# Residual adds of the down projection as accumulating DMAs, and one more block-product pair in the up projection

## The chip, the cores and the metric

The kernel runs on one NeuronCore of a Trainium2 chip. The metric is the device time of one execution in microseconds. The core has a matrix engine (TensorE, PE in the profile, with its weight loads as PEld), a vector engine (VectorE, DVE), a scalar engine (ScalarE, ACT), a general engine (GpSimd, POOL) and a queue that mostly issues DMAs (SyncE, SP). Each works through its own instructions in the order in which they were issued, and they meet at semaphores. Matrix products land in PSUM, everything else lives in SBUF.

## The reference

Two layers of an encoder trunk on 512 tokens of width 1024, all in float32. The first half of each layer (a gated recurrence, a spatial gate and a windowed attention, merged and added to `x`) is not touched. What matters is the second half:

```python
        hn = rms_norm(x, ln2[l])
        x = x + jnp.square(jax.nn.relu(hn @ w_up[l])) @ w_down[l]
    return rms_norm(x, final_norm)
```

`w_up` is 1024 x 4096 and `w_down` 4096 x 1024 per layer.

## The kernel before

**Precision.** Every operand of a float32 product is split into a high part `hi` (rounded to the matrix engine's fast float32 type) and a rest `lo`, and each product is three matmuls (`hi*hi`, `lo*hi`, `hi*lo`). For weights `wsplit` (L201) does this: `hi` is a ScalarE cast (L203), `lo` a VectorE subtraction (L204), both 128 x 1024, into one of `WB` = 3 pairs of buffers (`whl`, L197). `split` (L255) does the same for activations (L258, L259).

**The MLP in quarters.** The 4096 hidden features of a layer are taken in four quarters `qd` (loop at L1244). A quarter has an up part and a down part, and each hands its tiles to the next.

*Up*: eight tiles of 128 features, taken as four pairs `j`. A plain pair is two calls of `proj` (L212): per tile 8 x 3 matmuls of 512 columns with one split weight chunk, then Relu and Square on ScalarE (L1269, L1270). A block pair is one call of `up_pair` (L493): the two tiles together are a 2 x 2 block product done with seven block products instead of eight. Each has 4 x 3 matmuls of 256 columns, 84 in all. It has to form sums of the two raw weight chunks first (L499, L500, L503, L505, all VectorE, 512 wide), splits four weight tiles instead of two (three of 1024 columns, one of 512), and puts its results together with three VectorE adds (L529, L535, L537). `PAIRS[qd]` and `AHEAD[qd]` (L89) say which pairs are block products: none in quarter 0, pair 1 (whose weights are loaded ahead, into the `wq` buffers) and pair 2 (loaded into the `wr` buffers, of which there are `WR` = 2) in quarters 1 to 3. After each pair `left_first` and `left_second` (L360, L368) make the sums and splits of the hidden tiles that the down part needs.

*Down* (`down`, L471, through `seven`, L422): the quarter's 512 x 1024 hidden block times a 1024 x 1024 block of `w_down`, again as seven block products, in the order 1, 2, 6, 7, 5, 4, 3. Each is 24 matmuls of 512 columns into two PSUM banks (p = 0, 1). Before products 6, 5 and 4 VectorE forms sums of raw weight chunks in place (L447, L449, L451), two each. Later products add to what an earlier one left in the same bank (6, 5 and 3 on the banks of 1; 4 on those of 7), so each intermediate result has to be read out before the next product on that bank begins. The reading out is `on` (L474): one VectorE instruction per bank (L478), which takes the PSUM bank, multiplies it by the row scale `r2` (or its negative) and adds it to the residual tile `xr[t][fl]` in SBUF. There are 14 of these in a quarter. In quarter 3 `done` follows, which begins the next norm and the stores.

**Order.** The program is written once in plain order; a planner built into the framework lists the instructions of each engine by priority and by when its own model has their inputs ready. `hp()` raises a block's priority; among raised ones the earlier in the text goes first. The order on each engine is then fixed.

**Queues.** SP issues all weight loads (512 KB each). POOL issues the other loads and stores, and DMAs that do arithmetic; the descriptors of POOL's DMAs are kept in a strip of SBUF whose size the last function of the kernel sets (`dynamic_dma_scratch_size`, not given before).

Of the kernel before, what the change touches and what calls it, by code (L numbers as in the profile page):

```python
# [9 lines left out]
AF = mybir.ActivationFunctionType  # L10
ALU = mybir.AluOpType
# [48 lines left out]
def trunk(tc, xT, xt, ws, vec, fnb, bsb, snk, wst, rope, cmask, amask, ident, out):  # L60
    nc = tc.nc
# [3 lines left out]
    def pool(**kw):  # L65
# [15 lines left out]
             "yh": 8,  # L81
             "q": 2, "a": 8, "g": 2, "ch": 7,
             "yi": 16, "th": 8,
             "h": 18, "xm": 8}

    HOME = {t: p for p, ts in {"G": ("xs", "zt"), "Y1": ("yh",), "br": ("q", "a", "g", "ch"), "Y2": ("yi", "th"), "mlp": ("h", "xm")}.items() for t in ts}
    part = {}
    BANKS = {"m": 2, "a": 2, "c": 2, "s": 2}
    PAIRS, AHEAD = ((), (2,), (2,), (2,)), ((), (1,), (1,), (1,))  # L89
    GROUPS = (("m", "m", "c", "c"), ("a", "a", "s", "s"))  # L90
    WR, WB, NZ, NSM, NQ = 2, 3, 2, 3, 8

    CTS = {2: 5, 3: 4}

    def nm(s):
        ctr[0] += 1
        return f"{s}_{ctr[0]}"

    def T(tag, name, dt=F32):
        where = part[HOME[tag]] if tag in HOME else sb  # L100
        return where.tile([P, S], dt, tag=tag, bufs=SLOTS[tag], name=nm(name))
# [17 lines left out]
    def PT(tag, name):  # L119
        return ps.tile([P, S], F32, tag="p_" + tag, bufs=BANKS[tag], name=nm(name))  # L120
# [44 lines left out]
    pt = PT("s", "idle")  # L165
# [46 lines left out]
    def proj(xs, name, *key, bank="m"):  # L212

        return proj_w(xs, name, wload(*key), bank=bank)
# [256 lines left out]
    def down(qd, raw, hs, xr, r2, nr2, done, between, last):  # L471
        V = nc.vector

        def on(which, p, pt):  # L474
            t, fl, sign = {"P1": (p, 0, 1), "P2": (p, 0, 1), "P16": (2 + p, 0, 1), "P7": (2 + p, 1, -1),
                           "P165": (2 + p, 1, -1), "P74": (2 + p, 0, 1), "P1653": (p, 1, -1)}[which]
            r = r2 if sign > 0 else nr2
            V.scalar_tensor_tensor(xr[t][fl], pt, r[:, t:t + 1], xr[t][fl], ALU.mult, ALU.add)  # L478
            if qd == 3 and which in ("P2", "P165", "P74", "P1653"):
                done(t, fl)  # L480

        seven(raw, hs, "d", on, between=between, apart=last and qd == 3)
# [292 lines left out]
    for i in range(8):  # L775
        t = T("zt", "xt")
# [9 lines left out]
    for l in range(DEPTH):  # L786
        xs = n1.xs
# [164 lines left out]
        for g in range(4):  # L952
            pt = PT("s", "mx")
# [64 lines left out]
        pt = PT("c", "vT")  # L1018
# [69 lines left out]
        def gates(tag, i, fl):  # L1088

            res = []  # L1090
            for t in range(4):
                z = T(tag, "gt")
                nc.gpsimd.dma_start(z, thd[:, i * 4 + t, fl * S:(fl + 1) * S])
                res.append(z)
            return res
# [34 lines left out]
        with later(30000):  # L1130
# [5 lines left out]
            for fl in range(2):  # L1136
                th = gates("ch", 0, fl)
# [31 lines left out]
        for fl in range(2):  # L1169
            th, mc = tha[fl], mcs[fl]  # L1170
# [9 lines left out]
        xr = [[T("l", "xr"), T("l", "xr")] for _ in range(4)]  # L1180
# [47 lines left out]
        def done(t, fl):  # L1228

            n1.add(t, fl)  # L1230
            if not last:
                nc.gpsimd.dma_start(xspill[:, t, fl * S:(fl + 1) * S], xr[t][fl])
            if last:

                if fl == (t > 1):
                    nc.vector.tensor_tensor(xr[t][fl], xr[t][fl], fn_t[fl], ALU.mult)
                if (t, fl) in ((0, 1), (1, 1)):
                    finish((t,))
                elif (t, fl) == (3, 0):
                    finish((2, 3))  # L1240
            elif t % 2:
                n1.turn(fl, (t - 1, t))

        for qd in range(4):  # L1244
# [10 lines left out]
            for j in range(4):  # L1255
                if j in PAIRS[qd] or j in early:
                    us = up_pair(*(early.get(j) or pair_load(keys(j), False)), hx, "s" if j % 2 else "m")
                for i in range(2):
# [3 lines left out]
                    else:  # L1262
                        pt = proj(n2.xs, f'up{qd}', l, "up", qd, f, bank="s" if f % 4 > 1 else "m")
# [156 lines left out]
```

## Time and profile before

| | us |
|---|---|
| median of 3 runs | 1645.81 |
| lowest and highest run | 1644.52, 1646.4 |
| span of the profiled execution | 1644.4 |
| PE busy in it | 1631.2 (99%) |
| DVE, ACT, POOL busy in it | 1358.9 (83%), 1012.9 (62%), 102.4 (6%) |

The profile is that of one execution; its span counts from the first to the last instruction, and lies 1.4 us under the median of the runs. In the profile a matmul is shown with the time from its start to the end of its pipeline, so matmuls overlap, and what a matmul costs is the distance from one start to the next. VectorE instructions overlap their neighbours by a little in the same way. The eight quarters of the two layers lie at 495.3 to 821.2 us (layer 0) and 1312.1 to 1636.4 us (layer 1).

### The profile page before, as it was taken

The page shows a single profiled execution, that of the slowest core. Times are in us where ns is not written, and L with a number is a line of the kernel's source. Part 1 is how long each engine was busy: PE and PEld are TensorE (multiplying, and loading weights), DVE is VectorE, ACT ScalarE, POOL GpSimd, SP SyncE. Part 2 cuts the span into 40 slices and gives each one's busy share as a digit, 9 for nine tenths or more (in the row PEclk, how much of TensorE's full clock was granted, in tenths as well). Part 3 has the DMA queues.
Part 4 walks back from the last instruction along what each step waited for, and adds up shares of the span by engine and source line. Part 5 has one row for each costly group of instructions (what it writes and reads, how often), then busy time and mean ns, then how long its engine had stood idle before and what let it go on. Part 6 is the DMA issues. An engine that isn't in the chain of part 4 may idle for free. (4 is left out here: it accounts for less than half of the span.)

```text
span 1644.4 us, 24323 instructions
## 1 busy us (share of the span) xinstructions
PE 1631.2 (99%) x9137; PEld 1376.8 (84%) x9137; DVE 1358.9 (83%) x2183; ACT 1012.9 (62%) x1731; POOL 102.4 (6%) x165
## 2 busy tenths in 40 slices
PE   9999999999999999999999999999999999999998
PEld 7788888888888898989888888888887888989896
DVE  7888979677758988898989869887877589898887
ACT  7667567677247564646666555886862464647374
POOL 0012000000300000000010110000003000000001
PEclk9999999999999999999999999999999999999999
DMA  8343222222625333232423432223226343232311
GB/s 309 102 154 125 78 90 73 102 97 85 236 92 190 100 106 103 103 115 91 141 90 125 144 121 78 77 91 105 92 86 232 106 162 117 89 128 77 129 65 52
DMA packets 55590, 191.55 MB, mean 116 GB/s; under 512 B 7376, under 2 KB 7632, under 8 KB 55472
## 3 DMA queue, kind: packets, MB, share of 16 engines
q1 hardware_dynamic: 44352, 154.43, 27.3%
q0 software_dynamic: 10688, 35.00, 5.8%
q8 instruction: 72, 1.18, 0.3%
q10 hardware_dynamic: 432, 0.55, 0.1%
q14 instruction: 46, 0.38, 0.1%
HBM read 173.18 MB, written 16.78 MB: 116 GB/s over the span
## 5 line engine op out<-in xcount | busy, mean ns | idle before, releaser
L203 ACT CAST wh<-wq 128x1024 fp32r<-128x1024 f32 x214 | 225.2, 1053 | 205.1 <-PE dA L434 60.9
L204 DVE TENSOR_TENSOR wl<-wq,wh 128x1024 fp32r<-128x1024 f32 x214 | 260.4, 1221 | 62.8 <-ACT wh L203 60.3
L203 ACT CAST wh<-wr 128x1024 fp32r<-128x1024 f32 x164 | 172.0, 1049 | 155.1 <-PE wo L251 27.5
L204 DVE TENSOR_TENSOR wl<-wr,wh 128x1024 fp32r<-128x1024 f32 x164 | 199.9, 1220 | 61.0 <-ACT wh L203 55.1
L210 PE MATMUL up<-xh,wl 128*128 128x512 f32 x320 | 124.8, 390 | 0.0
L209 PE MATMUL up<-xl,wh 128*128 128x512 f32 x320 | 124.8, 390 | 0.0
L208 PE MATMUL up<-xh,wh 128*128 128x512 f32 x320 | 124.6, 391 | 0.0
L434 PE MATMUL dA<-wh,sh 128*128 128x512 f32 x256 | 99.8, 390 | 0.0
L433 PE MATMUL dA<-wh,sh 128*128 128x512 f32 x256 | 98.5, 390 | 0.0
L435 PE MATMUL dA<-wl,sh 128*128 128x512 f32 x256 | 91.9, 389 | 0.0
L656 DVE TENSOR_TENSOR ex<-ex 128x512 f32<-128x512 f32 x112 | 74.9, 686 | 3.5 <-ACT kt L647 3.2
L208 PEld LDWEIGHTS up<-xh,wh 128*128 128x128 f32 x320 | 60.1, 188 | 12.4
L210 PEld LDWEIGHTS up<-xh,wl 128*128 128x128 f32 x320 | 60.1, 188 | 12.3
L209 PEld LDWEIGHTS up<-xl,wh 128*128 128x128 f32 x320 | 60.1, 188 | 12.2
L644 ACT ACTIVATE qt<-ex 128x512 f32<-128x512 f32 x56 | 37.9, 677 | 33.8 <-DVE ex L656 31.8
L433 PEld LDWEIGHTS dA<-wh,sh 128*128 128x128 f32 x256 | 48.1, 188 | 10.0
L434 PEld LDWEIGHTS dA<-wh,sh 128*128 128x128 f32 x256 | 48.1, 188 | 9.9
L435 PEld LDWEIGHTS dA<-wl,sh 128*128 128x128 f32 x256 | 48.1, 188 | 9.9
L523 PE MATMUL us<-xs,wh 128*128 128x256 f32 x192 | 54.1, 283 | 0.0
L522 PE MATMUL us<-xs,wh 128*128 128x256 f32 x192 | 54.1, 283 | 0.0
L524 PE MATMUL us<-xs,wl 128*128 128x256 f32 x192 | 53.4, 283 | 0.0
L208 PE MATMUL gz<-xh,wh 128*128 128x512 f32 x128 | 50.9, 398 | 0.0
(435 smaller groups left out, 4780.6 us busy)
## 6 DMA issues: line engine op xcount, KB each, us to landing
wr<-in_ws_dram SPq DMA_DIRECT2D x158, 512.0 KB, 3.5
wq<-in_ws_dram SPq DMA_DIRECT2D x124, 512.0 KB, 4.3
thd<-zt POOLq DMA_DIRECT2D x32, 256.0 KB, 2.5
gt<-thd POOLq DMA_DIRECT2D x32, 256.0 KB, 3.9
mgd<-mg POOLq DMA_DIRECT2D x16, 256.0 KB, 2.3
mB<-mgd POOLq DMA_DIRECT2D x16, 256.0 KB, 6.7
x<-in_xT_dram SPq DMA_DIRECT2D x8, 256.0 KB, 7.5
xt<-in_xt_dram SPq DMA_DIRECT2D x8, 256.0 KB, 8.3
```

The lines of the kernel that those rows point to most:

```text
L203: nc.scalar.copy(hi, raw)
L204: nc.vector.tensor_tensor(lo, raw, hi.bitcast(F32), ALU.subtract)
L208: nc.tensor.matmul(pt, whi, xhi, start=first, stop=False)
L209: nc.tensor.matmul(pt, whi, xlo, start=False, stop=False)
L210: nc.tensor.matmul(pt, wlo, xhi, start=False, stop=last)
L433: nc.tensor.matmul(pt, xh[:, t], hi[:, c], start=start and k == 0, stop=False, skip_group_check=True)
L434: nc.tensor.matmul(pt, xl[:, t], hi[:, c], start=False, stop=False, skip_group_check=True)
L435: return nc.tensor.matmul(pt, xh[:, t], lo[:, c], start=False, stop=k == 3, skip_group_check=True)
L522: nc.tensor.matmul(pt, hi[:, c], xh, start=n in (1, 2, 7) and k == 0, stop=False, skip_group_check=True)
L523: nc.tensor.matmul(pt, hi[:, c], xl, start=False, stop=False, skip_group_check=True)
L524: nc.tensor.matmul(pt, lo[:, c], xh, start=False, stop=k == 3, skip_group_check=True)
L656: nc.vector.tensor_tensor(o_ap, o_ap, ap_of(ex, i_, [[istep, 2]] + z), ALU.add)
```

## The change

In quarters 0 to 2 of each layer the 14 results of a down part are no longer added to the residual by VectorE. ScalarE copies each PSUM bank with its scale into one of four new buffers `dx`, and a DMA issued from POOL adds that buffer to the residual tile. Quarter 3 is as it was. In quarters 1 to 3 pair 3 of the up part becomes a block pair as well (so pairs 1, 2 and 3 are), its weights loaded into the `wr` buffers, of which there are now 3. To make room in SBUF for `dx` (four tiles of 2 KB per partition) and the third `wr` (4 KB), the strip for POOL's DMA descriptors is set to 4 KB per partition.

```diff
-             "h": 18, "xm": 8}
+             "h": 18, "xm": 8, "dx": 4}
...
-    PAIRS, AHEAD = ((), (2,), (2,), (2,)), ((), (1,), (1,), (1,))
+    PAIRS, AHEAD = ((), (2, 3), (2, 3), (2, 3)), ((), (1,), (1,), (1,))
...
-    WR, WB, NZ, NSM, NQ = 2, 3, 2, 3, 8
+    WR, WB, NZ, NSM, NQ = 3, 3, 2, 3, 8
...
             r = r2 if sign > 0 else nr2
+            if qd < 3:
+                z = T("dx", "dx")
+                nc.scalar.activation(z, pt, AF.Copy, scale=r[:, t:t + 1])
+                nc.gpsimd.dma_start(xr[t][fl], z, accum_op=ALU.add)
+                return
             V.scalar_tensor_tensor(xr[t][fl], pt, r[:, t:t + 1], xr[t][fl], ALU.mult, ALU.add)
-            if qd == 3 and which in ("P2", "P165", "P74", "P1653"):
+            if which in ("P2", "P165", "P74", "P1653"):
                 done(t, fl)
...
-    nc = _bacc.Bacc("TRN2", target_bir_lowering=False, num_devices=1)
+    nc = _bacc.Bacc("TRN2", target_bir_lowering=False, num_devices=1, dynamic_dma_scratch_size=4096)
```

More of the change, by code (lines that the diff above doesn't have):

```diff
@@ L83, in trunk @@
              "yi": 16, "th": 8,
-             "h": 18, "xm": 8}
-    HOME = {t: p for p, ts in {"G": ("xs", "zt"), "Y1": ("yh",), "br": ("q", "a", "g", "ch"), "Y2": ("yi", "th"), "mlp": ("h", "xm")}.items() for t in ts}
+             "h": 18, "xm": 8, "dx": 4}
+    HOME = {t: p for p, ts in {"G": ("xs", "zt"), "Y1": ("yh",), "br": ("q", "a", "g", "ch"), "Y2": ("yi", "th"), "mlp": ("h", "xm", "dx")}.items() for t in ts}
     part = {}
     BANKS = {"m": 2, "a": 2, "c": 2, "s": 2}
-    PAIRS, AHEAD = ((), (2,), (2,), (2,)), ((), (1,), (1,), (1,))
+    PAIRS, AHEAD = ((), (2, 3), (2, 3), (2, 3)), ((), (1,), (1,), (1,))
     GROUPS = (("m", "m", "c", "c"), ("a", "a", "s", "s"))
-    WR, WB, NZ, NSM, NQ = 2, 3, 2, 3, 8
+    WR, WB, NZ, NSM, NQ = 3, 3, 2, 3, 8
     CTS = {2: 5, 3: 4}
```

## The prediction

> **What bounds the kernel now.** First the head of the page and its strip of 40 slices, then the list of what PE waited for.
>
> ```profile
> span 1644.4 us, 24323 instructions
> ...
> PE 1631.2 (99%) x9137; PEld 1376.8 (84%) x9137; DVE 1358.9 (83%) x2183; ACT 1012.9 (62%) x1731; POOL 102.4 (6%) x165
> ...
> DVE  7888979677758988898989869887877589898887
> ```
>
> ```profile
> PE idle L167 <- DVE idle L164: 1.6, 1, 1.6
> PE tA L435 <- DVE wl L204: 1.3, 1, 1.3
> PE wo L251 <- DVE mgl L259: 0.4, 2, 0.3
> ```
>
> PE is busy all the time and its longest waits are single ones in other stages: none lies on an up or a down matmul. So only PE work that goes away can shorten the MLP, and only a new PE wait can lengthen it. DVE is at 8 to 9 tenths in the MLP slices (13 to 20, 32 to 40): the engine that could make PE wait. Next, one late quarter of layer 1 by stretches (PE, PEld, DVE, ACT, POOL busy, clock, DMA share, GB/s): plain pair, block pairs 1 and 2, plain pair 3, products 1 and 2 of the down part; then the whole down parts of an earlier quarter and of the last.
>
> ```profile
> 1556.00:1566.90 10.90, 10.90 (x50) 9.03 (x49) 7.49 (x11) 3.20 (x6) 0.00 (x0) 1.00 0.25 94
> 1566.90:1577.00 10.10, 10.10 (x85) 10.07 (x84) 8.70 (x14) 6.99 (x12) 0.00 (x0) 1.00 0.32 105
> 1577.00:1587.70 10.70, 10.70 (x88) 10.55 (x87) 9.29 (x17) 9.17 (x17) 0.00 (x0) 1.00 0.31 98
> 1587.70:1598.20 10.50, 10.50 (x49) 8.69 (x48) 10.50 (x17) 7.43 (x15) 0.00 (x0) 1.00 0.16 52
> 1598.20:1609.00 10.80, 10.80 (x49) 8.97 (x48) 9.93 (x14) 6.94 (x9) 0.00 (x0) 1.00 0.00 0
> ...
> 620.90:659.00 38.10, 38.10 (x170) 31.57 (x169) 33.40 (x39) 17.57 (x20) 0.00 (x0) 1.00 0.34 113
> ...
> 1598.20:1636.40 38.20, 38.20 (x169) 31.32 (x167) 34.17 (x43) 20.59 (x32) 1.98 (x4) 1.00 0.01 2
> ```
>
> The reader is to see the fourth row: in the stretch of pair 3, which the change makes a block pair, DVE is already busy for all of its 10.50 us. It works off there what the two block pairs left behind.
>
> **What PE gains.** Three starts of that quarter: the plain pair, the first block pair, the down part.
>
> ```profile
> 1556.00 0.39 PE L208 MATMUL up<-xh,wh 128*128 128x512 f32 x1
> ...
> 1566.88 0.28 PE L522 MATMUL us<-xh,wh 128*128 128x256 f32 x1
> ...
> 1598.16 0.39 PE L433 MATMUL dA<-wh,sh 128*128 128x512 f32 x1
> ```
>
> A plain pair (48 matmuls) takes 1566.88 - 1556.00 = 10.88 us. From 1566.88 to 1598.16 are 31.28 us for two block pairs and one plain: (31.28 - 10.88) / 2 = 10.20 us for a block pair (84 matmuls). Making one more pair a block pair saves 0.68 us, and six of them (three quarters, two layers) 4.1 us, 0.25%. That is all that the change takes off PE; the DMAs and copies take no PE work away.
>
> **What DVE gets and loses.** DVE prices as the distance from one start to the next:
>
> ```profile
> 1573.30 1.22 DVE L204 TENSOR_TENSOR wl<-wr,wh 128x1024 fp32r<-128x1024 f32 x1
> 1574.43 0.69 DVE L259 TENSOR_TENSOR sh<-sf,sh 128x512 fp32r<-128x512 f32 x1
> 1575.04 0.69 DVE L499 TENSOR_TENSOR wr<-wr,wr 128x512 f32<-128x512 f32 x1
> 1575.64 0.41 DVE L535 TENSOR_TENSOR u<-u,us 128x256 f32<-128x256 f32 x1
> 1575.97 0.69 DVE L500 TENSOR_TENSOR wr<-wr 128x512 f32<-128x512 f32 x1
> ...
> 1578.37 0.69 DVE L259 TENSOR_TENSOR wl<-t,wh 128x512 fp32r<-128x512 f32 x1 [0.78 <-ACT wh L258]
> ```
>
> A `lo` of 1024 columns costs 1.13, a 512-wide sum or split 0.60, a 256-wide add 0.33 us. A block pair has, over a plain one, four sums (L499, L500, L503, L505) and one 512-wide split, 5 x 0.60 = 3.0; one more `lo`, 1.13; three adds, 1.0: 5.1 us more DVE work in each up part of quarters 1 to 3. What goes:
>
> ```profile
> 1599.22 1.23 DVE L204 TENSOR_TENSOR wl<-wq,wh 128x1024 fp32r<-128x1024 f32 x1 [0.87 <-ACT wh L203]
> ...
> 1600.72 1.22 DVE L451 TENSOR_TENSOR wq<-wq,wq 128x1024 f32<-128x1024 f32 x1
> 1601.85 0.42 DVE L383 SCALAR_TENSOR_TENSOR sf<-sf,u 128x256 f32<-128x256 f32 x1
> ...
> 1604.86 1.40 DVE L478 SCALAR_TENSOR_TENSOR xr<-dA,r,xr 128x512 f32<-128x512 f32 x2
> 1606.18 1.22 DVE L451 TENSOR_TENSOR wq<-wq,wq 128x1024 f32<-128x1024 f32 x1
> 1607.31 1.22 DVE L204 TENSOR_TENSOR wl<-wq,wh 128x1024 fp32r<-128x1024 f32 x1
> ```
>
> Two L478 cost 1.32, so 14 cost 9.2 us in each down part of quarters 0 to 2. That is more than comes, but in another place: it goes where PE did not wait, and work cannot be pulled forward to it, because `lo` needs one of three weight buffers, which PE frees at its own pace (the 0.87 us wait for a cast above is such a wait).
>
> So DVE enters the down part late, and the sharpest due time there is the weights of product 6. Its first `lo` (1607.31) ends at 1608.53, product 6 starts half a us later (1598.16 + 2 x 38.10 / 7 = 1609.05). In quarter 3 the lateness is 5.1 for the pair, plus 0.7 as PE comes earlier, less the 0.5 margin, less the 0.87 idle gap, less two L451 (2 x 1.13) that the planner can put behind, since only product 4 needs them: 2.2 us. Two splits of `left_second` may go behind too (0.9): 1.2 to 2.2 us. In quarters 1 and 2 the two L478 of product 1 are gone as well (1.32): 0 to 0.9. I take the middles, 0.4, 0.4 and 1.7 per layer, 5.0 us in both. After product 6 the last down part has work for DVE in 34.17 of 38.20 us and the others 9.2 less, so nothing later is due.
>
> **ScalarE, POOL and the DMAs.** The nearest rows for a copy out of PSUM, for DMAs from POOL, and for what POOL spends to issue one:
>
> ```profile
> L1269 ACT ACTIVATE u<-up x40: 582/590/606, 510.0 to 1599.1; 128x512 f32<-128x512 f32 x40
> ```
>
> ```profile
> thd<-zt POOLq DMA_DIRECT2D x32, 256.0 KB, 2.5
> ...
> mgd<-mg POOLq DMA_DIRECT2D x16, 256.0 KB, 2.3
> mB<-mgd POOLq DMA_DIRECT2D x16, 256.0 KB, 6.7
> ```
>
> ```profile
> L874 POOL DMA_DIRECT2D thd<-zt x32: 539/539/607, 83.8 to 963.7; - x32
> ```
>
> 14 copies of 0.59 are 8.3 us on ACT per down part: 17.57 becomes 26 of 38.10, which fits. A copy waits for its product's end; behind it in ACT's queue stand casts (L203) which wait for PE as well. I cost it at nothing; without that cover it is 1.2 us per product. The bank is needed again one product later at the earliest (38.10 / 7 = 5.44 us), so two copies have time. In the up part a block pair adds one and a half casts of 1024 columns and three copies of 256, at the 0.59 per 512 columns some 2.7 us, to ACT, which is the less loaded engine in every row above.
>
> No row shows an accumulating DMA. It moves 256 KB and reads its target too: from 2.3 us (a plain store) to 13.4 (twice the slowest load). I take 5.0, twice `thd<-zt`, the nearest in size and queue. Two DMAs on one residual tile must follow one another (products 1 and 2, 7 and 5), 5.44 us apart: 5.0 fits. Four `dx` tiles hold two products, 10.9 us: fits. POOL has nothing else in quarters 0 to 2, 14 issues of 0.54 fill 7.6 us of 38.1, and the next to touch the residual is the next quarter's down part, over 40 us later. The DMA engines are at 0.34. So zero, up to a landing time of 10.9 us. The third `wr` lets loads start earlier, in a place where PE does not wait: zero. The smaller strip matters only if POOL had to wait for room; at one DMA per 2.7 us I take zero.
>
> [...]
>
> **The rivals.**
>
> *A, DVE keeps up: faster.* DVE is idle for 1.4 us in each of the second and third stretches above (10.10 - 8.70, 10.70 - 9.29), 2.8 together, more than the 2.2 of quarter 3. If the new order fills those gaps, no due time is missed and the 4.1 us stay: 1641.7. Against it: those gaps wait for ACT casts inside a chain (the 0.78 above), and a third pair has the same chain.
>
> *B, PE waits inside the third pair: slower.* In 1577.0 to 1587.7 DVE worked 9.29 us. With a block pair next it must also make L499, L500 and L503 there (1.8 us): 11.1 us in 10.2, then comes the cast with its 0.78: 1.7 us late for the third pair's product 6. The `left` work of pair 2 comes first in the text, and if the planner puts part of it before that pair's last splits, more. It decides as soon as what DVE owes at the start of pair 3 is over 1 us. At 1.7 to 3 us in six quarters, 10 to 18 us, less 4.1: 1652 to 1660, most likely near its low end, 1653. The lateness at product 6 of the down part is then used up and not added.
>
> *C, the accumulating DMAs land late: slower.* Beyond 10.9 us a `dx` is not free, ACT stands still at the copy, and the casts behind it stop PE. At 13.4 us, 14 DMAs through 4 tiles need 47 us for a down part of 38: 9 us in six parts, +50, 1696. Against it: all POOL rows lie under 7 us. [...]
>
> **How the numbers follow.** The forecast: -4.1 + 5.0 = +0.9, 1645.3 for the profiled span and 1646.7 for the median, which lies 1.4 above it. Its own range is -4.1 + 2 x 1.2 = -1.7 to -4.1 + 2 x (0.9 + 0.9 + 2.2) = +3.9: 1644.1 to 1649.7. Chances: forecast 0.42, A 0.25, B 0.25, C 0.08. A measurement of this kernel tells about 0.2% (3.3 us) from no change. A gives 0.21 faster and 0.04 within (small losses are enough); the forecast 0.39 within and 0.03 slower; B and C 0.33 slower. So 0.21, 0.43, 0.36. The range runs from A with a little to spare, 1641, to the larger part of B, 1655; C and the end of B are left out.
>
> **What would show it.** PE has 9137 - 6 x 48 + 6 x 84 = 9353 matmuls. Right: waits of about 0.4 to 2 us of PE for DVE `wl` at the start of product 6 (second `dA` group), longest in quarter 3, and the three block pairs at 10.2 us each. A: no such waits. B: the waits stand at `us` in the third pair. C: ACT waits for a DMA on `dx`, and landings over 10 us. The prediction is wrong from the start if the order of the untouched stages shifts by more than a us or two.

## The result, and the profile after

| | before | after |
|---|---|---|
| median, us | 1645.6 | 1659.73 |
| lowest and highest run, us | 1644.52, 1646.4 | 1659.01, 1660.9 |
| span of the profiled execution, us | 1644.4 | 1659.1 |

The changed kernel is slower by 14.1 us: ratio 1.0088, 95% interval 1.0076 to 1.01. That lies outside the range given, above it. The head of the page of the changed kernel (busy time, share of the span and instructions of each engine):

```profile
span 1659.1 us, 25081 instructions
...
PE 1636.5 (99%) x9353; PEld 1384.5 (83%) x9353; DVE 1334.6 (80%) x2153; ACT 1074.4 (65%) x1851; POOL 174.7 (11%) x249
```

The amounts of work came out as worked out ahead: 9353 matmuls, and 1358.9 - 1334.6 = 24.3 us less busy time on DVE, against 6 x (9.2 - 5.1) = 24.6. Only the time went the other way. What PE waited for in the changed kernel (in total, times, longest):

```profile
PE us L529 <- DVE wl L204: 3.5, 6, 1.0
PE dB L433 <- ACT wh L203: 3.4, 6, 0.7
PE dC L433 <- ACT wh L203: 2.0, 1, 2.0
```

These three are new, are the longest and lie in the MLP: `us` L529 (the block pairs of the up part), `dB` (product 2 of the down part), `dC` (the banks of products 7 and 4, once). None of them stands at product 6 of the down part, where the prediction put the lateness. To see what each stage gained or lost, take the first matmul of a quarter and of the next: in the changed kernel, quarter 1 of layer 0,

```profile
577.27 0.39 PE L208 MATMUL up<-xh,wh 128*128 128x512 f32 x1
...
659.04 0.39 PE L208 MATMUL up<-xh,wh 128*128 128x512 f32 x1
```

and in the kernel before,

```profile
578.66 0.39 PE L208 MATMUL up<-xh,wh 128*128 128x512 f32 x1
...
658.96 0.39 PE L208 MATMUL up<-xh,wh 128*128 128x512 f32 x1
```

81.77 us against 80.30. In the same way, for all stages (us; "start" is what lies ahead of the first up part, "between" the untouched half of layer 1; the last quarter ends with the start of the last matmul, the tail with the span):

| | start | q0 | q1 | q2 | q3 | between | q0 | q1 | q2 | q3 | tail |
|---|---|---|---|---|---|---|---|---|---|---|---|
| before | 495.3 | 83.4 | 80.3 | 80.1 | 82.1 | 490.9 | 83.4 | 80.3 | 80.2 | 80.0 | 8.4 |
| after | 493.9 | 83.4 | 81.8 | 81.9 | 84.0 | 492.6 | 83.4 | 81.8 | 83.1 | 85.5 | 7.8 |

Quarter 0, which has the DMA adds and no block pair, is the same. The six quarters with a third block pair lose 1.5, 1.7, 2.0, 1.5, 2.9 and 5.5 us (from starts with two decimals), 15.0 together, where 4.1 were to be gained; the stretch between the layers loses 1.7; start and tail are 2.0 shorter.

**Where a quarter loses.** The changed kernel by stretches of quarter 1: block pairs 1, 2 and most of 3, then the start of the down part (PE, PEld, DVE, ACT, POOL busy, clock, DMA share, GB/s):

```profile
588.15:598.35 10.20, 10.20 (x86) 10.17 (x85) 8.77 (x14) 7.02 (x12) 0.00 (x0) 1.00 0.32 104
598.35:608.60 10.25, 10.25 (x86) 10.15 (x86) 9.21 (x17) 7.84 (x15) 0.00 (x0) 1.00 0.33 102
608.60:618.50 9.90, 9.48 (x75) 9.05 (x75) 9.90 (x17) 8.05 (x15) 0.00 (x0) 1.00 0.34 108
618.52:631.85 13.33, 12.64 (x61) 10.05 (x60) 13.18 (x20) 10.41 (x17) 0.85 (x1) 1.00 0.00 1
```

The reader is to see the third of the engine columns, DVE: 8.77, then 9.21, then 9.90 of 9.90. From the third block pair on DVE has no gap left, and there PE's column falls below the length for the first time. The instructions that waited there:

```profile
613.68 0.39 PE L529 MATMUL us<-xs,wl 128*128 128x256 f32 x1 [0.42 <-DVE wl L204]
...
618.60 1.05 ACT L203 CAST wh<-wq 128x1024 fp32r<-128x1024 f32 x1 [1.03 <-PE us L528]
...
621.77 1.05 ACT L203 CAST wh<-wq 128x1024 fp32r<-128x1024 f32 x1 [0.53 <-PE us L528]
...
622.87 0.50 PE L433 MATMUL dB<-wh,sh 128*128 128x512 f32 x1 [0.60 <-ACT wh L203]
```

First the third pair's product 7 waits for the `lo` of its weights. Then ScalarE cannot cast the down part's weights: each cast needs one of the three weight buffers, and waits for a matmul of the third pair (L528) to let go of it. The first of the two casts waits for the buffer of products 5 and 4. The second waits for that of products 7 and 3, and product 3 is the pair's last; PE starts it only at 620.27, after six matmuls of the down part's product 1. So PE waits again, for the cast of product 2. From one matmul's start to the next, less the usual spacing, PE loses some 0.6 us at product 7, 0.25 at product 1 (at 619.70, right behind the first of the two casts) and 0.9 at product 2. The whole quarter loses 1.47 + 0.68 = 2.15; the rest is in steps of about 0.1. Reckoned in the same way, quarter 2 of layer 0 loses 2.4, and quarters 1 and 2 of layer 1 lose 2.2 and 3.5. In the last of these, product 6 of the third pair waits 0.6 us for its `lo` as well, and product 7 waits 1.0.

**The last quarter.** What held `dC` up for 2.0 us in the last down part, in order of time:

```profile
1630.47 0.68 DVE L1241 TENSOR_TENSOR xr<-xr,fn 128x512 f32<-128x512 f32 x1
...
1631.07 1.22 DVE L449 TENSOR_TENSOR wq<-wq,wq 128x1024 f32<-128x1024 f32 x1
...
1632.38 1.99 ACT L203 CAST wh<-wq 128x1024 fp32r<-128x1024 f32 x2 [1.34 <-DVE wq L449]
...
1634.42 0.50 PE L433 MATMUL dC<-wh,sh 128*128 128x512 f32 x1 [2.02 <-ACT wh L203]
```

A weight sum (L449) stands on DVE behind the final norm's product (L1241), the first of the two casts waits for the sum, and PE for the second, which stands behind it. In the kernel before, this sum stands behind that product too, but there it ended 1.9 us before product 5 (PE, 1619.92), and here 0.9 us after product 5 began (1631.34):

```profile
1616.78 1.21 DVE L449 TENSOR_TENSOR wq<-wq,wq 128x1024 f32<-128x1024 f32 x1
```

So it is not this order that is new, but that DVE is late. This quarter keeps its residual adds on DVE, which comes into it late. By stretches around that wait:

```profile
1631.00:1634.50 3.50, 1.49 (x8) 0.91 (x6) 3.50 (x5) 2.02 (x3) 0.00 (x0) 1.00 0.00 0
1634.50:1638.50 4.00, 4.00 (x11) 3.14 (x12) 2.51 (x3) 0.00 (x0) 0.00 (x0) 0.57 0.00 0
1638.50:1642.00 3.50, 3.50 (x17) 2.91 (x16) 2.08 (x3) 1.51 (x2) 0.00 (x0) 1.00 0.00 0
```

Behind the five engine columns stands the granted clock: 1.00 in the first and the last row, 0.57 in the second, right behind the wait. The matmuls of that row, from the timeline, the third after the wait and the first at the usual spacing again; eight start from the one to the other:

```profile
1634.99 0.63 PE L433 MATMUL dC<-wh,sh 128*128 128x512 f32 x1
...
1638.40 0.39 PE L434 MATMUL dA<-wh,sh 128*128 128x512 f32 x1
```

That is 3.41 us for eight, 0.43 each, where 38.10 / 168 = 0.227 is usual: 1.6 us lost beside the wait's own 2.0. A wait of this length need not bring that on. The run with the third buffer only inside the MLP (below) has the same wait, and full clock right behind it:

```profile
1633.40 0.50 PE L433 MATMUL dC<-wh,sh 128*128 128x512 f32 x1 [2.02 <-ACT wh L203]
...
1633.50:1637.50 4.00, 4.00 (x18) 3.31 (x19) 2.67 (x4) 1.06 (x1) 0.00 (x0) 1.00 0.00 0
```

The other three runs of the changed kernel have a mean clock of 0.999 where the profiled one has 0.998, and spans of 1657.2 to 1658.3 us in place of 1659.1. So those 1.6 us belong to the profiled execution, and not to the change as such.

**The DMA adds.** All that reads or writes `dx` in the changed kernel (instructions with their durations in ns; who waited; landing):

```profile
L480 ACT ACTIVATE dx<-dA,r x48: 683/690/694, 544.4 to 1569.3; 128x512 f32<-128x512 f32 x48
...
ACT dx L480: 13.3, 10
...
DMA to landing us min/median/max: 3.1/6.1/10.9
```

A copy takes 0.69 us, a landing 6.1 in the median, at most 10.9. ScalarE waited 13.3 us for a free `dx`, in ten places, and quarter 0 did not get longer by it.

### The profile page after: what moved, and what is told of

Same layout as the page of the kernel before. It is cut to its first block, busy times and chain, and to the rows that moved or that the text cites. A ratio compares the mean times of both kernels' runs of the same rounds, so it can differ in the third digit from the quotient of the medians.

```text
span 1659.1 us, 25081 instructions
## 1 busy us (share of the span) xinstructions
PE 1636.5 (99%) x9353; PEld 1384.5 (83%) x9353; DVE 1334.6 (80%) x2153; ACT 1074.4 (65%) x1851; POOL 174.7 (11%) x249
## 5 line engine op out<-in xcount | busy, mean ns | idle before, releaser
L481 POOL DMA_DIRECT2D xr<-dx x84 | 72.0, 918 | 425.9 <-ACT dx L480 369.9
L209 PE MATMUL up<-xl,wh 128*128 128x512 f32 x224 | 87.3, 390 | 0.0
L210 PE MATMUL up<-xh,wl 128*128 128x512 f32 x224 | 87.3, 390 | 0.0
L208 PE MATMUL up<-xh,wh 128*128 128x512 f32 x224 | 86.5, 389 | 0.0
L529 PE MATMUL us<-xs,wl 128*128 128x256 f32 x288 | 81.1, 285 | 4.1 <-DVE wl L204 3.5
L527 PE MATMUL us<-xs,wh 128*128 128x256 f32 x288 | 81.1, 283 | 0.0
L528 PE MATMUL us<-xs,wh 128*128 128x256 f32 x288 | 81.1, 283 | 0.0
L527 PE MATMUL us<-xh,wh 128*128 128x256 f32 x216 | 61.7, 288 | 0.0
L528 PE MATMUL us<-xl,wh 128*128 128x256 f32 x216 | 60.5, 283 | 0.0
L529 PEld LDWEIGHTS us<-xs,wl 128*128 128x128 f32 x288 | 54.6, 191 | 5.5 <-DVE wl L204 4.7
L433 PEld LDWEIGHTS dA<-wh,sh 128*128 128x128 f32 x256 | 48.3, 189 | 13.0 <-ACT wh L203 3.3
L529 PE MATMUL us<-xh,wl 128*128 128x256 f32 x216 | 57.2, 283 | 0.0
```

The lines of the kernel that those rows point to most:

```text
L208: nc.tensor.matmul(pt, whi, xhi, start=first, stop=False)
L209: nc.tensor.matmul(pt, whi, xlo, start=False, stop=False)
L210: nc.tensor.matmul(pt, wlo, xhi, start=False, stop=last)
L433: nc.tensor.matmul(pt, xh[:, t], hi[:, c], start=start and k == 0, stop=False, skip_group_check=True)
L527: nc.tensor.matmul(pt, hi[:, c], xh, start=n in (1, 2, 7) and k == 0, stop=False, skip_group_check=True)
L528: nc.tensor.matmul(pt, hi[:, c], xl, start=False, stop=False, skip_group_check=True)
```

## The experiments

Times are medians; "over before" is against runs of the kernel before on the same chip.

### One part alone: the DMA adds, the third pair, the third raw buffer

*The DMA adds and copies alone* (the pairs as before):

```diff
-    PAIRS, AHEAD = ((), (2, 3), (2, 3), (2, 3)), ((), (1,), (1,), (1,))
+    PAIRS, AHEAD = ((), (2,), (2,), (2,)), ((), (1,), (1,), (1,))
-    WR, WB, NZ, NSM, NQ = 3, 3, 2, 3, 8
+    WR, WB, NZ, NSM, NQ = 2, 3, 2, 3, 8
```

> The ScalarE copies and accumulating DMAs of quarters 0 to 2 alone: pairs as in the kernel before (1 and 2), two wr buffers. Theory S (supply: the third block pair needs four split weight tiles in 10.2 us through three buffers, and VectorE and ScalarE do not keep up; the DMAs cost PE nothing): the time of before within 2 us, quarters 1 and 2 at 80.3 us each from up start to up start as before. Theory D (the accumulating DMAs, 6.1 us to landing, hold up ScalarE and with it the casts): at least 7 us over before, with PE waits for wh casts in quarters 1 and 2.

1644.55 us, 0.6 below before, ratio 0.9996 (0.9987 to 1.0005): no difference. Copies, DMAs and strip cost nothing, and the 55 us (6 x 9.2) that they take off VectorE give nothing either, as PE did not wait for it.

*The third pair alone* (VectorE adds the results; three `wr`):

```diff
-            if qd < 3:
+            if qd < 0:
                 z = T("dx", "dx")
...
-            if which in ("P2", "P165", "P74", "P1653"):
+            if qd == 3 and which in ("P2", "P165", "P74", "P1653"):
```

> The third block pair alone: residual adds on VectorE in all quarters as before, three wr buffers. Theory S: slower than before by 10 to 25 us, as VectorE has 9.2 us more in each of six down parts than in the changed kernel. Theory D: the 4.1 us gain of the pair shows, less a little lateness: from 4 us faster to 5 us slower.

1664.36, ratio 1.0115 (1.01 to 1.013), +19.2. The loss is the pair's. It is larger than that of the whole change, and the waits say where:

```profile
PE dC L433 <- ACT wh L203: 5.3, 5, 2.0
PE dB L433 <- ACT wh L203: 3.5, 6, 0.7
PE us L529 <- DVE wl L204: 2.8, 6, 0.5
```

The wait of `dC` comes five times in place of once. So the DMA adds are worth something exactly where VectorE is already late: some 5 us here, nothing by themselves.

*The third raw buffer alone* (the kernel before, with `WR` = 3 and the 4 KB strip that makes room):

```diff
-    WR, WB, NZ, NSM, NQ = 2, 3, 2, 3, 8
+    WR, WB, NZ, NSM, NQ = 3, 3, 2, 3, 8
```

> The kernel before with three wr buffers and the 4 KB strip, nothing else. Theory S (all of the loss is in the third pair and what follows it): the time of before within 2 us, the stretch between the layers 490.9 us as before. Theory R (the third wr buffer makes the planner order the untouched stages worse): the stretch between the layers 492.5 to 494 us, 2 to 4 us over before in all.

1652.69, ratio 1.0042 (1.0027 to 1.0057), +6.9. 5.8 of it lie between the layers (496.7 in place of 490.9), and the last quarter is 1.4 longer. First the kernel before at the start of that stretch, an instruction of ScalarE, then a window:

```profile
825.46 0.82 ACT L335 ACTIVATE xf<-xT,vec_t 128x256 f32<-128x256 f32 x2
```

```profile
828.00:832.00 4.00, 4.00 (x20) 3.27 (x19) 1.47 (x8) 2.90 (x6) 2.84 (x3) 1.00 0.78 227
```

Then the same two views with three buffers:

```profile
825.97 1.98 ACT L203 CAST wh<-wr 128x1024 fp32r<-128x1024 f32 x2
827.85 0.82 ACT L335 ACTIVATE xf<-xT,vec_t 128x256 f32<-128x256 f32 x2
```

```profile
826.00:828.00 2.00, 1.35 (x9) 0.90 (x7) 2.00 (x6) 2.00 (x4) 0.00 (x0) 1.00 0.53 215
828.00:832.00 4.00, 1.08 (x5) 0.68 (x6) 3.07 (x8) 2.56 (x7) 3.00 (x3) 1.00 0.78 222
832.00:836.00 4.00, 4.00 (x13) 3.10 (x13) 3.94 (x11) 3.34 (x8) 0.29 (x1) 0.57 0.82 289
```

With a raw chunk more at hand, two weight casts in a row stand ahead of the evacuation of the transposes (L335), which comes 2.4 us later (827.85 for 825.46). PE is idle for 0.65 + 2.92 us and the clock falls to 0.57 behind it. A buffer more changed the order of a stage that the edit doesn't touch.

*The change with two raw buffers*, and *with the third one only inside the MLP* (a tile of its own for pair 3's first chunk):

```diff
-    WR, WB, NZ, NSM, NQ = 3, 3, 2, 3, 8
+    WR, WB, NZ, NSM, NQ = 2, 3, 2, 3, 8
```

```diff
-    def pair_load(key, ahead):
+    def pair_load(key, ahead, third=False):
...
+                r = part["mlp"].tile([P, CW], F32, tag="w3", bufs=1, name=nm("wr")) if third and n == 0 else part["wq"].tile([P, CW], F32, tag="wq", bufs=NQ, name=nm("wq")) if ahead else sb.tile([P, CW], F32, tag="wr", bufs=WR, name=nm("wr"))
...
+                    us = up_pair(*(early.get(j) or pair_load(keys(j), False, j == 3)), hx, "s" if j % 2 else "m")
```

> The changed kernel with two wr buffers in place of three. Theory S: the third pair's raw weights come later by one buffer, so its sums wait for a load: 14 to 20 us over before. Theory R: the stretch between the layers goes back to 490.9 us and quarter 3 gains too: 10 to 13 us over before.

> The changed kernel with two wr buffers, and a tile that exists only in the MLP for the first weight chunk of pair 3, so that pair 3 has its three raw buffers and the other stages have two as before. Theory R (the third wr buffer costs time where other stages use it): the stretch between the layers goes from 492.6 back to 490.9 us and the time to 11 to 13 us over before; the quarters 1 and 2 stay at 81.8 us. Rival (the third buffer's cost in e8 does not add to that of the pair): the changed kernel's 14 over before, within 1.

1669.85 (1.0149, 1.0133 to 1.0164) and 1659.08 (1.0087, 1.0069 to 1.0105). With two buffers the third pair's weights come late:

```profile
PE us L527 <- DVE sh L259: 5.9, 6, 1.0
PE us L527 <- ACT wh L203: 3.3, 7, 0.7
```

The first row names a split of the hidden tiles, because that ended last. In quarter 1 of layer 0 the cast of the pair's summed weights (`wh<-t`, L258) ended at 613.14, product 6 started at 613.20, and it is these weights that it reads.

With the buffer in the MLP alone the stretch between the layers is 491.6, 1.0 shorter than the change's, and the total is the same. So what the third buffer costs by itself is hardly there in the full change, and does not add to what the pair costs. Nor does the stretch need that buffer to grow: with pairs 1 and 3 and two buffers (below) it is 492.5.

### Why the pair loses: buffers, sums, activations

*A split buffer of its own for the third pair's weights of products 7 and 3*, once in the kernel with the pair alone and once in the change (with two `wr`, three `dx` and a strip of 2 KB, for room):

```diff
+    def whe():
+        return (part["mlp"].tile([P, CW], F32R, tag="eh", bufs=1, name=nm("wh")),
+                part["mlp"].tile([P, CW], F32R, tag="el", bufs=1, name=nm("wl")))
...
-                    w3 = wsplit(r1)
+                    w3 = wsplit(r1, own)
...
```

> The third pair without the DMA adds (as in e2), and the split weight tile that the third pair's first and last late products share gets a buffer of its own in the MLP, so that it does not hold one of the three. Theory Sb (the held buffer keeps the casts of products 1 and 2 back): the waits of 0.25 and 0.9 us there go in six quarters, 6 to 7 us less than e2's 19.2 over before, so 12 to 13 over. Theory Sw (VectorE and ScalarE have too much work, the buffer only names the place): the wait moves to a later product, within 2.5 us of e2.

> The whole change with the same buffer of its own; for room two wr, three dx and a strip of 2 KB. Its twin is e9. Theory Sb: 6 to 7 us less than e9, some 7 us over before. Theory Sw: within 2.5 us of e9.

The first: 1659.11 (1.0081, 1.0066 to 1.0096), 5.9 us better over before than without that buffer, of which some 4 us lie in the six quarters by the profiles. The wait of `dB` is gone, others took its place (the lines of this run lie 4 further down):

```profile
PE dA L437 <- ACT sh L262: 4.4, 6, 0.9
PE us L531 <- ACT wh L207: 4.0, 6, 0.7
```

The second: 1677.02 (1.0196, 1.0179 to 1.0213), 7.2 worse than the change with two `wr`, the opposite. Most of that is the clock: in the trace it is 0.50 for some 3.4 us in each of the six quarters, against two such stretches in the change with two `wr`. Four more at the 1.6 us measured in the last quarter above are 6.4 us, an estimate. The run differs in `dx` and strip too, so it doesn't tell whether the buffer helps there. The held buffer is a part of the loss, not its bottom.

*A fourth split buffer everywhere* (two `wr`, two `dx`):

```diff
-             "h": 18, "xm": 8, "dx": 4}
+             "h": 18, "xm": 8, "dx": 2}
-    WR, WB, NZ, NSM, NQ = 3, 3, 2, 3, 8
+    WR, WB, NZ, NSM, NQ = 2, 4, 2, 3, 8
```

> The changed kernel with four pairs of split weight buffers (WB = 4) in place of three; to make room two wr and two dx buffers. Theory S, if the buffers are what is short: the PE waits for wh at product 2 (0.9 us in six quarters) and most of those for wl inside the third pair (0.6 to 1.1 us each) go, 6 to 10 us less than the changed kernel, 4 to 8 us over before. If it is VectorE's sum of work and not the buffers: within 3 us of the changed kernel. Theory D: with two dx buffers ScalarE waits for landings more often: 16 us or more over before.

1704.42 (1.0368, 1.035 to 1.0385), the worst of all, and inconclusive: the stages that the edit doesn't name lost too (504.3 at the start, 504.1 between the layers), and two `dx` are too few. A part of the former is the clock: it is 0.50 for 10.2 us at the start and for 13.7 us between the layers, worth at most half of that, some 5 and 7 of the 9 and 13 us lost (an estimate: in the last quarter above 1.6 of 3.41 us were lost at 0.50). The waits of the down part:

```profile
PE dC L433 <- ACT dx L480: 6.1, 4, 2.6
...
PE dA L433 <- ACT dx L480: 4.5, 4, 2.0
```

PE waits 10.6 us for copies that wait for a landed DMA. That is the case of late landings among the rivals of the prediction, reached by halving the tiles.

*No weight sums in the third pair* (its four sums on VectorE left out; the output differs), and *no Square in pairs 2 and 3* (left out on ScalarE; the output differs):

```diff
+            if bare:
+                split(r0[:, lo_], w2[0][:, lo_], w2[1][:, lo_])
+            else:
                 V.tensor_tensor(r0[:, lo_], r0[:, lo_], r1[:, lo_], ALU.add)
...
```

```diff
-                    A.activation(u, u, AF.Square)
+                    if not bare:
+                        A.activation(u, u, AF.Square)
...
```

> The changed kernel, but pair 3 leaves its four raw weight sums out (2.4 us of VectorE in each of six quarters; the output is another one). Theory Tv (VectorE's work in and around the third pair is what PE waits for): the 2.2 us that each quarter 1 and 2 loses against the pair's gain go almost wholly, those quarters fall to 80 us, and the time to 1 to 6 us over before. Theory Ta (ScalarE's casts, copies and activations are): within 3 us of the changed kernel.

> The changed kernel, but pairs 2 and 3 leave their Square out (four ScalarE instructions of 0.53 us in each of six quarters, 2.1 us; the output is another one). Theory Ta: quarters 1 and 2 fall by 1 us or more and the time to 5 to 9 us over before. Theory Tv: within 3 us of the changed kernel.

Without the sums 1652.85 (1.0042, 1.0027 to 1.0057): 6.5 us less over before than the change, quarters 1 and 2 at 80.8 in place of 81.8 and more. Without the squares 1659.99 (1.0089, 1.0073 to 1.0105): nothing gained in the time. In its profile quarters 1 and 2 are 0.6 to 0.8 us shorter than in the change (81.1 in layer 0), while quarter 3 of layer 0 is 0.7 and the stretch between the layers 1.0 longer, so the order moved the loss elsewhere. The sums, 2.4 of the 5.1 us that the pair adds on VectorE, and the waits that hang on them are nearly half of the loss, 6.5 of 14.1. What is left without the sums:

```profile
PE dC L433 <- ACT wh L203: 2.0, 1, 2.0
PE dB L433 <- ACT wh L203: 1.9, 6, 0.3
...
PE us L532 <- DVE wl L204: 1.4, 6, 0.2
```

### Place or number

*No third pair in quarter 3:*

```diff
-    PAIRS, AHEAD = ((), (2, 3), (2, 3), (2, 3)), ((), (1,), (1,), (1,))
+    PAIRS, AHEAD = ((), (2, 3), (2, 3), (2,)), ((), (1,), (1,), (1,))
```

> The changed kernel with pair 3 of quarter 3 plain again in both layers. Theory S: quarter 3 goes back to its length of before (82.1 and 80.4 us), and with it the 1.7 us between the layers: 1645.6 + 14.1 - 1.9 - 5.5 - 1.7, some 5 us over before; quarters 1 and 2 stay 1.5 to 2.9 us longer each. Theory D: there are no accumulating DMAs in quarter 3, so nothing is cured there but the pair's own gain is lost: at least 12 us over before.

1655.31 (1.0062, 1.0047 to 1.0077), between the two expectations: the last quarter falls from 85.5 to 81.4, quarters 1 and 2 stay at 81.8, and 493.8 between the layers pointed to the third raw buffer.

*One block pair, pair 3, in quarter 0*, beside the DMA adds with two `wr`; *pair 2 there instead*; and *pairs 1 and 3 as block pairs in quarters 1 to 3*, pair 2 plain:

```diff
+    PAIRS, AHEAD = ((3,), (2,), (2,), (2,)), ((), (1,), (1,), (1,))
```

```diff
+    PAIRS, AHEAD = ((2,), (2,), (2,), (2,)), ((), (1,), (1,), (1,))
```

```diff
+    PAIRS, AHEAD = ((), (3,), (3,), (3,)), ((), (1,), (1,), (1,))
```

> The accumulating DMAs of e1 (two wr, pairs 1 and 2 in quarters 1 to 3), and pair 3 of quarter 0 as its first and only block pair, with plain pairs before it. If a block pair pays where it follows plain ones: quarter 0 goes from 83.4 to 82.7 us in both layers, 1.4 us less than e1, 1643.5. If the pair's weights come late there too: 1 to 3 us more than e1.

> The DMA adds and copies with two wr buffers, and one block pair more in quarter 0 of each layer, pair 2, followed by a plain pair. P: quarter 0 goes from 83.4 to 82.7 us, 1.4 us off in both: 1643.1. N (a block pair after plain ones costs there what pair 3 cost in quarter 0): 84.4 in quarter 0, 1647.

> The DMA adds and copies with two wr buffers, and two block pairs in quarters 1 to 3 as before, but pairs 1 and 3: pair 2 is plain and a block pair stands directly before the down part. P: each of the six quarters loses what pair 3 lost in quarter 0, 0.7 + 1.0 = 1.7 us: 81.9 in place of 80.2, 1654.7. N (the number counts, not the place): quarters of 80.2, 1644.5.

Pair 3 in quarter 0: 1647.0 (1.001, 1.0001 to 1.002), 2.3 us more over before than the DMA adds alone; the quarter takes 84.4 us in place of 83.4, though its three other pairs are plain. Pairs 1 and 3: 1653.19 (1.0049, 1.0036 to 1.0061), with no more work than the kernel with the DMA adds alone, and 8.1 us more over before. Quarters 1 and 2 are at 80.9 for 80.2, the last quarters at 84.1 and 82.5 for 82.1 and 80.0, and of the three waits of the change two are there again, while that inside the third pair is gone:

```profile
PE dB L433 <- ACT wh L203: 1.9, 6, 0.3
PE dC L433 <- ACT wh L203: 1.9, 2, 1.0
```

So the place alone costs: a block pair directly before the down part is a loss, even where nothing else is added. Pair 2 in quarter 0 fell out for a reason that neither expectation named: 1661.69 (1.0097, 1.0083 to 1.0111), the quarter at 91.4:

```profile
PE us L527 <- ACT xs L258: 8.3, 2, 4.1
```

PE waits some 4.1 us in each layer for `xs`, the split sums of the activations, which a quarter later are ready, and behind the wait the clock is 0.50 for 6.8 us in layer 0 and 10.2 in layer 1. The run says nothing on place or number.

*Three block pairs in quarters 1 to 3, but pairs 0, 1 and 2*, so that a plain pair stays before the down part, with two `wr` and with three:

```diff
+    PAIRS, AHEAD = ((), (0, 2), (0, 2), (0, 2)), ((), (1,), (1,), (1,))
...
+                    sq = A.activation(v, v, AF.Square)
+        return u, v, sq
...
+                    if j == 0:
+                        mark = us[2]
```

> The DMA adds and copies with two wr buffers, and three block pairs in quarters 1 to 3 as in the change, but pairs 0, 1 and 2: the plain pair stays directly before the down part. The work of PE, VectorE and ScalarE is that of the change; only the place differs. Theory P (the place before the down part is what costs): each of the six quarters is up to 0.68 us shorter than with two block pairs, 79.5 to 80.2 in place of 81.8 to 85.5; 1640.5 to 1644.5 us. Rival N (three block pairs in an up part are more than VectorE and the weight buffers carry, wherever they stand): quarters of 83 us and more as with the change and two wr buffers, 1665 or more.

> The same with three wr buffers. P: the run with two, plus up to the 6.9 us that the third buffer cost by itself, mostly in the stretch between the layers: 1641 to 1651. N: near the change, 1657 or more.

1667.14 (1.0129, 1.0113 to 1.0144) and 1663.7 (1.0108, 1.0094 to 1.0122): the times are the rival's, not those of the theory that only the place matters. Quarter 1 with two `wr`, block pairs 0 and 2 and the whole down part:

```profile
577.66:588.40 10.74, 8.97 (x73) 8.69 (x72) 9.55 (x13) 5.61 (x10) 1.73 (x2) 1.00 0.75 178
...
599.00:609.80 10.80, 10.48 (x84) 10.00 (x83) 10.44 (x20) 9.23 (x17) 0.00 (x0) 1.00 0.30 101
622.56:660.64 38.08, 38.08 (x170) 31.53 (x168) 28.08 (x33) 24.09 (x32) 9.66 (x12) 1.00 0.68 175
```

The down part runs clean again (38.08 of 38.08), as the place theory says; but PE is idle for 1.8 us in the first pair, and VectorE is at 10.44 of 10.80 in the third, so the gain is spent there. In the first pair it is an order, on VectorE:

```profile
575.18 1.23 DVE L420 TENSOR_TENSOR wq<-wq,wq 128x1024 f32<-128x1024 f32 x1 [3.39 <-DMA wq<-in_ws_dram]
576.32 1.22 DVE L204 TENSOR_TENSOR wl<-wr,wh 128x1024 fp32r<-128x1024 f32 x1
```

The early sums of the down part's weights (L420, two of them) stand ahead of pair 0's sums, and the first waits 3.39 us for a load. Before a plain pair that costs nothing. So the rival's times came about in part for another reason than the rival's. Whether three block pairs would pay without those two instructions in that place was not tried.

No version was found that beats the kernel before by more than a measurement tells.

## Why the prediction was wrong, step by step

- *What bounds the kernel* (PE; only a new wait can lengthen the MLP): right. Every loss found is a wait of PE, or a lower clock behind one.
- *0.68 us gained per block pair*: right in size. Block pair 1 takes 598.35 - 588.15 = 10.20 us in the changed kernel too. It is paid only where the pair is fed.
- *VectorE 5.1 more in each up part, 9.2 less in three down parts of four*: right, 24.3 us less for 24.6.
- *"So DVE enters the down part late, and the sharpest due time there is the weights of product 6"*: **this is the step that failed.** Being late was right; the due time was not. It came earlier: at the third pair's product 7 and at products 1 and 2 of the down part, 2.2 to 3.5 us per quarter where 0.4 stood (quarters 1 and 2), 2.6 and 6.2 where 1.7 stood (quarter 3). Two things were overlooked. The backlog was counted on VectorE alone, while the chain from sum to cast to `lo` runs over two engines and has no gap to catch up in; the row of 9.90 in 9.90 us was in reach from the 9.29 of pair 2 and the sums due next, a sum that rival B does and the forecast leaves out. And a buffer was taken to come free at PE's own pace, while the third pair holds one until its last product, just as the down part needs two new tiles. Leaving out the pair's sums took 6.5 of the 14 us away; giving it a buffer of its own took 5.9 (some 4 in the quarters), where VectorE still made the residual adds; moving a pair to that place without adding one cost 8.1.
- *The last quarter*, 1.7 us: undersized. Against before it lost 2.0 us in layer 0 and 5.5 in layer 1, the latter by the sum behind the final norm's work (2.0) and the clock behind that wait (1.6, which another run with the same wait did not have). "So nothing later is due" was wrong there: product 5's sum was due, and late. The two `L451` "that the planner can put behind" weren't the ones in question: L449 was late.
- *DMAs and copies cost zero*: right, with 1644.55 for them alone. The landing of 6.1 us was taken as 5.0; the longest, 10.9, is just the bound set for zero. POOL took 0.85 us (median) to issue one, where 0.54 was taken. The copy took 0.69 where 0.59 was taken.
- *The third `wr`, zero*: wrong by itself (6.9), and small in the change (of the 1.7 us between the layers 1.0 went when that buffer was confined to the MLP, and 1.6 are there with two buffers and pairs 1 and 3). The argument looked at where loads start in the MLP, and not at what a raw chunk more lets the planner put ahead in other stages. As a whole the untouched stages shifted by 1.4, 1.7 and 0.6 us, within the "us or two" beyond which the prediction called itself wrong from the start.
- *The rivals*: B named the engine, the pair and a price of 1.7 to 3 us per quarter; of quarters 1 and 2 three lost 2.2 to 2.4, inside it, and one 3.5. Its range ended at 1660, the result is 1659.73. That the total fits is luck in part: B put the wait at product 6, where PE waited in one quarter only, and had no wait in the down part, where about half of quarter 1's loss lies; and 3.6 us of the profiled span are the wait and the clock in the last quarter. It was also written down as most likely near its low end, and the range given cut off the rest. C did not happen with four `dx`. A's gaps on VectorE (1.4 us per block pair) are 1.4 and 1.0 in pairs 1 and 2 and gone in pair 3.

What stays open: why quarter 2 of layer 1 has the further wait at product 6, how the loss divides between the pair's sums, the held buffer and the order (no run takes all of it away), and why four split buffers bring waits into stages that the pairs don't touch.

## What to carry to other kernels

A step that saves PE time paid here only where its feeding engines had room next to it (six more block pairs, worth 4.1 us, made their quarters 15.0 longer; VectorE was busy for 9.90 of 9.90 us in the one shown): sum their work over the stretch in which it is consumed, through the whole chain (sum, cast, `lo`, buffer), and look for the first due time after it, not the sharpest. Work taken off an engine in another stretch helped only where the engine was late there: the DMA adds were worth 5 us beside the third pair and nothing without it. And a buffer more was not free in a planned order (6.9 us by itself): look at the stages that share it.

## What the hardware showed that was not expected

- A wait of PE cost more here than its length. After 2.0 us of idleness the granted clock was 0.57 over the next 4 us, a further 1.6 us; in another run, after the same wait, it stayed at 1.00. In the run with three raw buffers the 0.57 came after two waits, of 1.0 and 2.6 us. What decides between the two outcomes was not tried. Inside a kernel, the clock records of the traces have a stretch of 3.41 us at 0.50 in the changed kernel, and of 6.83 and 10.24 us in the run with pair 2 in quarter 0, there behind waits of 4.1 us.
- An accumulating DMA of 256 KB within SBUF took 3.1 to 10.9 us to land, 6.1 in the median, against 2.5 in the kernel before, and 3.4 in the changed one, for the plain store of that size (`thd<-zt`) from the same queue.
